# Encoder block on one core: own buffers for the bias tables, result stores by head pair, wider value products

## The chip, the cores and the metric

The kernel runs on one core of a Trainium2 chip. A core has five engines with instruction queues of their own: TensorE (PE; its weight loads are shown apart as PEld), VectorE (DVE), ScalarE (ACT), GpSimd (POOL) and SyncE (SP, which here issues most DMAs). PE writes to PSUM, eight banks of 512 float32 columns in each of 128 partitions; the other memory on the core is SBUF. The metric is the time of one execution on the device in microseconds; lower is better.

## The reference, cut to what matters

One layer of an encoder: 2048 tokens, width 1024. After a norm, one projection feeds two attention mixers; their outputs are normed, concatenated and projected, and an expert layer and a last norm follow. The change lies in the two mixers and in what prepares them.

```python
# mixer A: 8 heads x 64, three patterns (window, dilation) = (128,1), (512,4), (2048,16)
rel_steps = np.arange(span)[None, :] - half_steps - np.arange(qb)[:, None]
bias = rel_bias[t5_relative_bucket(rel_steps * dilation)].transpose(2, 0, 1)
scores = where(valid, q @ k.T * dh ** -0.5 + bias, NEG_INF)      # keys i + j*dilation, |j| <= 64
m, p = max(scores), exp(scores - max(scores)); l = sum(p)
o, lse = p @ v / l, m + log(l)
out_a = sum over patterns of softmax(lse over patterns) * o
# mixer B: 8 heads, every query against every key
sc = (q_nope @ k_nope.T + q_rope @ k_rope.T) * 96 ** -0.5
out_b = softmax(sc) @ v
```

## The kernel before, in words

Products that need float32 accuracy are made of two halves: a value is split into a high part and its residue (the low part), and high x high, high x low and low x high are added up in PSUM. The order of instructions on every engine is the order in which the program emits them.

**Phase 1** (`phase1`) goes over 16 token tiles of 128 tokens. For tile c the loop emits `stage_b(c + 1)` (eight transposes of the normed tile into PSUM, ACT takes the high part, DVE the residue, L153 to L156), `stage_a(c + 3)` (the norm: ACT's squares, some ten small DVE instructions, one DVE scaling, L136 to L141, and the load of x two tiles on), steps of work done on the side, and `stage_c(c)` (24 products of 416 columns for mixer B's latents, L163). The transposes use the PSUM pool `pt` of two banks, the projections `pm` of four.

Work on the side: `bias_tables` builds mixer A's biases. After a load step and a one-hot step it makes eight tables for pattern 1 (`y`, 496 columns each, two per step), two parts for pattern 4 (384 and 288 columns) and one for pattern 16 (256). Each table is two products of 8 rows (L397, L398) into a bank of `pt`, a DVE copy to an SBUF area `b` (L399) and a store to DRAM by SP; the pattern-1 results alternate between two slots of `b`. `vb_scale` loads mixer B's value weights and works out a power-of-two scale for them; `vscale` does so for mixer A's. `chain` makes one sequence of `bias_tables` and `vb_scale`, and a dictionary says how many steps of it a tile takes: one at tiles 0, 2, 6 and 7, two at 3, 4, 5 and 8. The one-hot tables lie in the columns 1024 to 2048 of `hT[0]`, which later tiles fill.

Then come the v and the q and k projections, held in `hT`, with stores to DRAM.

**Mixer A** (`phase3`) takes the 8 heads one after the other, 20 units a head: 4 of pattern 16, then 8 of pattern 1, then 8 of pattern 4. It is a pipeline over steps s, where a unit passes through `qk` (PE), `soft1` (DVE: adds the bias and takes the row minimum of the negated scores into column 65 of the result tile, L604), `soft2` (POOL subtracts it), `soft3` (ACT's exp), `trans` (PE, ACT), `low` (DVE) and `pv` (PE; ACT then copies the values and the sum of weights of a group of units into columns 0 to 64 of the result tile, L685), each a step after the one before; `pv` runs five steps behind `qk`. At unit 1 of a head SP is given the loads of the next head's q and k (six loads of 0.5 MB), at unit 5 of an even head the v of the next pair.

The result tile `st` holds a head's 48 windows, 66 columns each, from a pool of two buffers. When `pv` has done a head's last unit, which is step 4 of the next head, SP gets eight stores of that head (L723 to L728) into DRAM `na`, where a token's row in a pattern is 8 heads x 66 numbers: every piece is 264 bytes long. A new tile from a pool waits until everything that used the buffer before is done, stores included; `soft1` at the start of a head waits so on DVE.

**Mixer B** (`mla`) works in 256 steps, each with two key tiles for 512 queries of a head: six score products of 512 columns, two products for a later row maximum (DVE reduces it, L796), two ACT exps, residues on DVE and POOL (L833, L834), and the value products, two steps' worth at every second step. For each of 2 key tiles and 4 query tiles there are three: the high weights with the values' 65 columns (64 high parts and a one, L848), the same weights with the 64 low parts (L850), the low weights with the 65 (L852); all three add into the same 65 columns of one bank. After eight steps ACT copies the bank (260 columns) to `os`, DVE works out the reciprocal of the sum, POOL multiplies into `ob`, and SP stores it (L855 to L862).

## Time and profile before

| | us |
|---|---|
| median of the runs shown | 2385.11 |
| lowest and highest of them | 2384.35, 2390.85 |
| the profiled execution | 2390.16 |
| its span, first to last instruction | 2388.1 |

| stretch of the profiled execution | us |
|---|---|
| phase 1, token tiles | 0 to 150 |
| phase 1, v, q and k projections | 150 to 440 |
| mixer A | 440 to 750 |
| mixer B with its preparation | 750 to 1578 |
| output projection, router, experts, last norm | 1578 to 2388 |

The profile is one execution on the chip. Busy times of engines are sums over instructions; of TensorE it also tells the clock granted to it, as a share of full speed, where 1.00 is 2.4 GHz and 0.50 is 1.2 GHz. A releaser, the event that ended an engine's wait, is inferred from semaphore events; where an instruction waits for several things, the last of them by the profile is named, and this can be another than the one that really held it.

### The profile page before, as it was taken

Reading aid. Unit: us, or ns where it says so; the run is one execution under the profiler, and the core shown is the slowest. Engines: PE = TensorE matmul, PEld = TensorE weight load, DVE = VectorE, ACT = ScalarE, POOL = GpSimd, SP = SyncE. Lnnn points to the kernel's source line nnn. Section 1 sums busy time; section 2 is a strip of 40 time slices with the busy share of each in tenths; the row PEclk is TensorE's granted clock in tenths of the full one; section 3 lists DMA queues with packets and bytes.
Section 4 is the critical chain, followed back from the end, with each engine's and each line's share of the span. In section 5 each row is a group of like instructions: output and inputs, shape, how many; then the busy total and the mean of one; then the engine's idle time right before and its main releaser. Section 6 shows DMA issues by size and latency. Waiting matters only on the chain. (4 is left out here: it accounts for less than half of the span.)

```text
span 2388.1 us, 45937 instructions
## 1 busy us (share of the span) xinstructions
PE 2156.3 (90%) x17613; PEld 1826.4 (76%) x17613; DVE 1624.7 (68%) x3584; ACT 1358.1 (57%) x2103; POOL 1075.7 (45%) x1137
## 2 busy tenths in 40 slices
PE   6799998788799999999999999989898799999990
PEld 5689886688788788888888887777676588788870
DVE  6542211457677788888888889877887677777764
ACT  4331111568678577777777776844343376667763
POOL 0110000346465245555555547454654666677740
PEclk8899999979789899999999999989999899999995
DMA  4322446999999300000000022135444598899978
GB/s 140 116 73 66 165 181 170 202 209 160 180 154 140 105 19 6 22 22 6 22 12 15 21 52 87 42 90 169 143 143 168 168 313 277 295 295 324 313 208 299
DMA packets 221776, 333.99 MB, mean 140 GB/s; under 512 B 113849, under 2 KB 165986, under 8 KB 205476
## 3 DMA queue, kind: packets, MB, share of 16 engines
q1 hardware_dynamic: 191508, 195.41, 32.9%
q0 software_dynamic: 29760, 134.85, 17.6%
q8 instruction: 140, 2.29, 0.4%
q14 instruction: 80, 0.66, 0.1%
q10 hardware_dynamic: 288, 0.79, 0.1%
HBM read 248.24 MB, written 109.64 MB: 150 GB/s over the span
## 5 line engine op out<-in xcount | busy, mean ns | idle before, releaser
L834 POOL TENSOR_TENSOR lo<-p,hi 128x512 f16<-128x512 f32 x256 | 359.1, 1403 | 315.8 <-ACT p L828 310.2
L796 DVE TENSOR_REDUCE part<-M 128x1 f32<-128x512 f32 x512 | 347.3, 686 | 50.6 <-PE M L794 48.1
L827 ACT ACTIVATE hi<-S 128x1024 f16<-128x1024 f32 x256 | 261.9, 1023 | 209.7 <-PE S L822 209.5
L828 ACT ACTIVATE p<-S 128x1024 f32<-128x1024 f32 x256 | 261.0, 1019 | 0.0
L833 DVE TENSOR_TENSOR lo<-p,hi 128x512 f16<-128x512 f32 x256 | 204.2, 798 | 9.8
L848 PEld LDWEIGHTS <-hi 128*128 128x128 f16 x2048 | 190.0, 97 | 26.2 <-issue 25.8
L852 PE MATMUL O<-VB,lo 128*128 128x65 f16 x2048 | 204.9, 193 | 5.4 <-DVE lo L833 3.1
L848 PE MATMUL O<-VB,hi 128*128 128x65 f16 x2048 | 206.4, 194 | 0.0
L850 PE MATMUL O<-VB,hi 128*128 128x64 f16 x2048 | 205.6, 196 | 0.0
L620 POOL TENSOR_TENSOR pp<-sb,st 128x512 f32<-128x512 f32 x32 | 33.4, 1049 | 363.3 <-DVE st L604 357.1
L852 PEld LDWEIGHTS <-lo 128*128 128x128 f16 x2048 | 191.5, 100 | 6.0 <-DVE lo L833 3.6
L850 PEld LDWEIGHTS <-hi 128*128 128x128 f16 x2048 | 191.4, 97 | 0.3
L626 POOL TENSOR_TENSOR pp<-sb,st 128x256 f32<-128x256 f32 (+1 forms) x256 | 143.0, 580 | 51.7 <-DVE st L604 41.7
L1972 DVE TENSOR_TENSOR s<-raw,s 128x1024 fp32r<-128x1024 f32 x120 | 140.1, 1220 | 12.8 <-ACT s L1970 12.6
L1929 PE MATMUL pd<-s,hT 128*128 128x512 f32 x540 | 138.3, 404 | 1.7 <-ACT hT L1916 1.7
L2016 POOL DMA_INDIRECT d_x<-o,rec x47 | 90.6, 1928 | 105.3 <-ACT s L1970 28.1
L1280 PE MATMUL pm<-s,mT_hi 128*128 128x512 f32 x512 | 135.2, 411 | 0.0
L303 DVE SCALAR_TENSOR_TENSOR qk_sb<-pm,qkscale,qk_sb 128x512 fp32r<-128x512 f32 x32 | 24.0, 751 | 162.8 <-ACT qk_sb L302 156.5
L654 ACT ACTIVATE phi<-PT 128x512 f16<-128x512 f32 (+1 forms) x160 | 96.0, 600 | 53.6 <-PE PT L643 52.4
L1929 PEld LDWEIGHTS pd<-s,hT 128*128 128x128 f32 x540 | 101.2, 188 | 30.1 <-issue 4.3
L578 PE MATMUL S<-KA,QA 128*128 128x256 f32 (+2 forms) x384 | 117.4, 329 | 7.5 <-issue 7.5
L604 DVE CUSTOM_DVE_ANT_0 sb<-S,t 128x128 f32<-128x128 f32 (+1 forms) x240 | 72.4, 349 | 75.5 <-PE S L579 37.7
(467 smaller groups left out, 6390.3 us busy)
## 6 DMA issues: line engine op xcount, KB each, us to landing
x<-in_x SPq DMA_DIRECT2D x32, 512.0 KB
d_qk<-qk_sb SPq DMA_DIRECT2D x64, 256.0 KB
na<-d_na SPq DMA_DIRECT2D x48, 264.0 KB
QA<-d_qk SPq DMA_DIRECT2D x16, 512.0 KB
KA<-d_qk SPq DMA_DIRECT2D x16, 512.0 KB
KB<-d_qk SPq DMA_DIRECT2D x16, 512.0 KB
d_x<-x SPq DMA_DIRECT2D x16, 512.0 KB
d_h<-h SPq DMA_DIRECT2D x16, 512.0 KB
```

The source lines that it names most:

```text
L626: nc.gpsimd.tensor_sub(dst, src, st[h][:, s0 + i, 65:66, None, None].to_broadcast([128, 2, na, nx // 2]))
L796: nc.vector.tensor_reduce(part[m][:, qt, kc:kc + 1], ps, axis=AX.X, op=ALU.max)
L827: nc.scalar.activation(hi, ps, AF.Exp)
L828: nc.scalar.activation(p32, ps, AF.Exp)
L833: nc.vector.tensor_sub(lo[:, :, 0:LV], p32[:, :, 0:LV], hi[:, :, 0:LV])
L834: nc.gpsimd.tensor_sub(lo[:, :, LV:512], p32[:, :, LV:512], hi[:, :, LV:512])
L848: nc.tensor.matmul(o[:, qt], hi[:, j, q], V[:, 0:65], start=(kt == 0 and qt == 0), stop=False, skip_group_check=True)
L850: nc.tensor.matmul(o[:, qt, 0:64], hi[:, j, q], V[:, 65:129], start=False, stop=False, skip_group_check=True)
L852: nc.tensor.matmul(o[:, qt], lo[:, j, q], V[:, 0:65], start=False, stop=(kt == 15 and qt == 3), skip_group_check=True)
L1280: nc.tensor.matmul(ps[half], mT[a][:, j], wo[b][j // 2][:, j % 2, 512 * half:512 * half + 512], start=(n == 0), stop=(n == 23))
L1929: self.nc.tensor.matmul(ps[:, half], hT[a][:, j], w[b][:, j, 512 * half:512 * half + 512], start=(n == 0), stop=(n == len(k) - 1))
L1972: eng.tensor_sub(lo, src, hi)
```

## The change

Three edits that touch different stretches.

First, the bias tables take their PSUM from a pool of their own, `p1tb`, two banks, and their steps are one per tile at tiles 0 and 2 to 8 (the tables themselves fall on tiles 3 to 8; with the one-hot step at tile 2 this is seven tiles). The four steps of `vb_scale` go beside them, at tiles 2, 4, 5 and 6, and still use `pt`. The pattern-1 results alternate among four slots of `b`, and the pattern-4 and pattern-16 results move within it. The one-hot tables lie from column 1280 on, since they are read up to tile 8. The fetch of the first value weights at tile 8 is emitted after the table step.

Second, mixer A's results are kept for a head pair and a pattern: a tile [128, 16 windows, 2 heads, 66] for each of the three patterns, one buffer each, in the same SBUF space as before. `put` stores a pattern when `pv` has done its last unit in the odd head: pattern 16 at step 8 of the odd head (one store), pattern 1 at step 16 (three), pattern 4 at step 4 of the next head (four). A piece in DRAM is 2 x 66 numbers, 528 bytes.

Third, in mixer B the three first query tiles take their 65 columns and the 64 low parts in one product of 129 columns, each query tile having 129 columns of the bank; the fourth keeps two products, since the bank has 512 columns. The copy to `os` takes 452 columns, POOL adds the low sums to the high ones for three query tiles, and the multiplication is done in place in `os`.

```diff
--- before.py
+++ after.py
...
             vs = vscale()
-            ahead = chain(self.bias_tables(rawp, hT[0][:, :, 1024:2048], pt), self.vb_scale(rawp, pt, sm))
+            tb = c1.enter_context(tc.tile_pool(name="p1tb", bufs=2, space=PSUM))
+            tables = self.bias_tables(rawp, hT[0][:, :, 1280:2048], tb)
+            vb = self.vb_scale(rawp, pt, sm)
...
+                if c in (10, 11, 12, 13, 14):
+                    next(vs, None)
+                if c in (0, 2, 3, 4, 5, 6, 7, 8):
+                    next(tables, None)
+                if c in (2, 4, 5, 6):
+                    next(vb, None)
                 if c == 8:
                     fetch(0)
                     fetch(1)
-                if c in (10, 11, 12, 13, 14):
-                    next(vs, None)
-                for _ in range({0: 1, 2: 1, 3: 2, 4: 2, 5: 2, 6: 1, 7: 1, 8: 2}.get(c, 0)):
-                    next(ahead, None)
...
         for y in range(8):
-            sl = b[:8, (y % 2) * 496:(y % 2) * 496 + 496]
+            sl = b[:8, (y % 4) * 496:(y % 4) * 496 + 496]
             table(o1[:, 0:31, 7 - y:23 - y], 496, sl)
             nc.sync.dma_start(AP(dr["t1"], y * 496, [[8 * 496, 8], [1, 496]]), sl)
             if y % 2:
                 yield
...
-        v4 = b[:8, 1000:1672]
+        v4 = b[:8, 0:672]
...
-        v16 = b[:8, 1700:1956]
+        v16 = b[:8, 992:1248]
...
-            ot = ctx.enter_context(tc.tile_pool(name="p3o", bufs=2))
+            ot = ctx.enter_context(tc.tile_pool(name="p3o", bufs=1))
...
-            SLOT = {pw: n for n, pw in enumerate((pat, w) for pat in (16, 4, 1) for p, ws in units if p == pat for w in ws)}
+            SLOT = {(pat, w): n for pat in (16, 4, 1) for n, w in enumerate(w for p, ws in units if p == pat for w in ws)}
...
+            def results(h, pat):
+
+                if (h // 2, pat) not in st:
+                    st[h // 2, pat] = ot.tile([128, 16, 2, 66], F32, name=f"st{pat}")
+                return st[h // 2, pat][:, :, h % 2]
+
+            def put(p, pat):
+
+                so = st.pop((p, pat)).rearrange("p w h n -> p w (h n)")
+                out = lambda w0, step, n: AP(dr["na"], w0 * 128 * 528 + p * 132, [[528, 128], [step * 128 * 528, n], [1, 132]])
+                if pat == 16:
+                    nc.sync.dma_start(out(0, 1, 16), so)
+                elif pat == 4:
+                    for i, t in enumerate((0, 3, 1, 2)):
+                        nc.sync.dma_start(out(16 + t, 4, 4), so.rearrange("p (r t) n -> p r t n", t=4)[:, :, i])
+                else:
+                    nc.sync.dma_start(out(33, 1, 14), so[:, 2:16])
+                    nc.sync.dma_start(out(32, 1, 1), so[:, 0:1])
+                    nc.sync.dma_start(out(47, 1, 1), so[:, 1:2])
 
...
-                if h not in st:
-                    st[h] = ot.tile([128, 48, 66], F32, name="st")
+                res = results(h, pat)
...
-                        accum_out=st[h][:, SLOT[pat, w], 65:66])
+                        accum_out=res[:, SLOT[pat, w], 65:66])
...
-                                         st[h][:, s0:s0 + nw, 65:66].to_broadcast([128, nw, n]))
+                                         res[:, s0:s0 + nw, 65:66].to_broadcast([128, nw, n]))
...
-                    nc.scalar.activation(st[h][:, idx:idx + nw, 0:65], ps[:, :nw], AF.Copy)
+                    nc.scalar.activation(results(h, pat)[:, idx:idx + nw, 0:65], ps[:, :nw], AF.Copy)
...
                     h, u = divmod(s - 5, U)
-                    if u == U - 1:
-                        so = st.pop(h)
-                        out = lambda w0, step, n: AP(dr["na"], w0 * 128 * 528 + h * 66, [[528, 128], [step * 128 * 528, n], [1, 66]])
-                        nc.sync.dma_start(out(0, 1, 16), so[:, 0:16])
-                        for i, t in enumerate((0, 3, 1, 2)):
-                            nc.sync.dma_start(out(16 + t, 4, 4), so[:, 16:32].rearrange("p (r t) n -> p r t n", t=4)[:, :, i])
-                        nc.sync.dma_start(out(32, 1, 1), so[:, 32:33])
-                        nc.sync.dma_start(out(47, 1, 1), so[:, 33:34])
-                        nc.sync.dma_start(out(33, 1, 14), so[:, 34:48])
+                    if h % 2 and u in (3, 11, 19):
+                        put(h // 2, {3: 16, 11: 1, 19: 4}[u])
...
-                    state["O"] = psO.tile([128, 4, 65], F32, name="O")
+                    state["O"] = psO.tile([128, 512], F32, name="O")
...
+
                         q = slice(128 * qt, 128 * qt + 128)
-                        nc.tensor.matmul(o[:, qt], hi[:, j, q], V[:, 0:65], start=(kt == 0 and qt == 0), stop=False,
-                                         skip_group_check=True)
-                        nc.tensor.matmul(o[:, qt, 0:64], hi[:, j, q], V[:, 65:129], start=False, stop=False,
-                                         skip_group_check=True)
-                        nc.tensor.matmul(o[:, qt], lo[:, j, q], V[:, 0:65], start=False, stop=(kt == 15 and qt == 3),
-                                         skip_group_check=True)
+                        c0 = 129 * qt
+                        own = 129 if qt < 3 else 65
+                        nc.tensor.matmul(o[:, c0:c0 + own], hi[:, j, q], V[:, 0:own], start=(kt == 0 and qt == 0),
+                                         stop=False, skip_group_check=True)
+                        if own == 65:
+                            nc.tensor.matmul(o[:, c0:c0 + 64], hi[:, j, q], V[:, 65:129], start=False, stop=False,
+                                             skip_group_check=True)
+                        nc.tensor.matmul(o[:, c0:c0 + 65], lo[:, j, q], V[:, 0:65], start=False,
+                                         stop=(kt == 15 and qt == 3), skip_group_check=True)
                 if kp == 7:
-                    os = wk.tile([128, 4, 65], F32, name="os", bufs=1)
-                    nc.scalar.activation(os, o, AF.Copy)
+                    os = wk.tile([128, 4, 129], F32, name="os", bufs=1)
+                    nc.scalar.activation(os.rearrange("p a n -> p (a n)")[:, 0:452], o[:, 0:452], AF.Copy)
+                    nc.gpsimd.tensor_add(os[:, 0:3, 0:64], os[:, 0:3, 0:64], os[:, 0:3, 65:129])
                     rl = sm.tile([128, 4, 1], F32, name="rl")
                     nc.vector.reciprocal(rl, os[:, :, 64:65])
                     nc.vector.tensor_scalar(rl, rl, vinv, None, op0=ALU.mult)
-                    ob = wk.tile([128, 4, 64], F32, name="ob", bufs=1)
-                    nc.gpsimd.tensor_mul(ob, os[:, :, 0:64], rl.to_broadcast([128, 4, 64]))
+                    ob = os[:, :, 0:64]
+                    nc.gpsimd.tensor_mul(ob, ob, rl.to_broadcast([128, 4, 64]))
                     nc.sync.dma_start(AP(dr["ob"], 4 * n * 128 * 512 + h * 64, [[512, 128], [128 * 512, 4], [1, 64]]), ob)
```

## Rows read from the trace of the kernel before

**Rows 1.** The page's second part, the span in 40 slices of 59.7 us each: busy tenths of PE, the granted TensorE clock in tenths of full speed, and the share of the DMA engines.

```profile
PE   6799998788799999999999999989898799999990
PEclk8899999979789899999999999989999899999995
DMA  4322446999999300000000022135444598899978
```

**Rows 2.** Stretches of the token-tile loop of phase 1, cut where the projections of tiles 2, 5, 9 and 12 begin (33.6, 80.4, 109.2 and 125.3 us). Columns: stretch and its length, busy time of PE, PEld, DVE, ACT and POOL (with instruction counts), granted clock, DMA share, GB/s.

```profile
33.60:80.40 46.80, 29.57 (x121) 21.95 (x119) 25.55 (x68) 12.47 (x34) 5.08 (x24) 0.75 0.22 66
80.40:109.20 28.80, 24.39 (x132) 23.20 (x131) 14.84 (x47) 11.77 (x35) 3.38 (x18) 0.93 0.33 100
109.20:125.30 16.10, 16.10 (x98) 15.87 (x96) 12.89 (x44) 12.66 (x28) 3.36 (x18) 1.00 0.82 269
```

**Rows 3.** PE in order of time, 40 to 66 us: table products (L397 and L398). Columns: start and duration in us, line, what; in brackets the idle time before it and its releaser.

```profile
41.99 0.42 PE L397 MATMUL pT<-hT_hi 33*8 33x496 f32 x1 [2.77 <-DVE hT_lo L156]
...
42.59 0.42 PE L397 MATMUL pT<-hT_hi 33*8 33x496 f32 x1
...
46.66 0.58 PE L397 MATMUL pT<-hT_hi 33*8 33x496 f32 x1 [3.39 <-DVE raw L399]
...
63.23 0.58 PE L397 MATMUL pT<-hT_hi 33*8 33x496 f32 x1 [3.72 <-DVE raw L399]
```

**Rows 4.** DVE in order of time, 38 to 90 us, the same columns: the first instruction of a norm chain (L46), the scaling by it (L141), the copies of a pair of tables (L399), and the residues of two transposes (L156).

```profile
42.46 0.14 DVE L46 TENSOR_SCALAR rs_t<-ss 128x1 f32<-128x1 f32 x1
...
44.74 1.28 DVE L141 SCALAR_TENSOR_TENSOR xn<-x,ss,g_attn 128x1024 f32<-128x1024 f32 x1
45.95 1.24 DVE L399 COPY raw<-pT 8x496 f32<-8x496 f32 x2
50.10 1.24 DVE L399 COPY raw<-pT 8x496 f32<-8x496 f32 x2 [2.92 <-DMA d_t<-raw]
57.49 1.29 DVE L156 TENSOR_TENSOR hT_lo<-pT,hT_hi 128x512 fp32r<-128x512 f32 x2 [6.15 <-ACT hT_hi L155]
```

**Rows 5.** Stretches of mixer A, columns as in rows 2: head 0; then (from a table of the heads one after the other, 441.0 to 745.8 us) head 6, head 7 and the sum; then, from a table without the idle time at heads' starts, heads 2 and 3.

```profile
441.00:486.80 45.80, 30.69 (x345) 29.04 (x345) 24.70 (x113) 25.70 (x51) 21.86 (x36) 0.82 1.06 210
...
679.90:714.20 34.30, 31.97 (x389) 31.31 (x390) 27.12 (x117) 25.44 (x53) 22.09 (x36) 0.82 1.02 121
714.20:745.80 31.60, 29.13 (x413) 27.79 (x411) 28.79 (x118) 28.88 (x60) 21.32 (x35) 1.00 1.06 142
sum 304.80, PE 256.97 PEld 248.44 DVE 216.38 ACT 223.91 POOL 175.55; mean PE 32.12 PEld 31.06 DVE 27.05 ACT 27.99 POOL 21.94
525.50:557.30 31.80, 29.98 (x387) 29.20 (x387) 27.16 (x116) 24.97 (x53) 21.75 (x36) 0.89 1.16 134
561.20:590.20 29.00, 27.77 (x393) 26.64 (x392) 27.06 (x116) 26.72 (x57) 21.67 (x36) 1.00 1.11 228
```

**Rows 6.** DVE in order of time: the first bias addition (L604) of heads 2, 3, 4 and 6, with the idle time before it and its releaser as the trace infers it, and, between them in time, the first one of pattern 4 in head 3 (step 12 of that head).

```profile
525.50 0.29 DVE L604 CUSTOM_DVE_ANT_0 sb<-S,t 128x128 f32<-128x128 f32 x1 [3.49 <-DMA QA<-d_qk]
...
561.27 0.29 DVE L604 CUSTOM_DVE_ANT_0 sb<-S,t 128x128 f32<-128x128 f32 x1 [4.03 <-DMA d_na<-st]
...
579.44 0.36 DVE L604 CUSTOM_DVE_ANT_1 sb<-S,t 128x192 f32<-128x192 f32 x1
...
611.78 0.29 DVE L604 CUSTOM_DVE_ANT_0 sb<-S,t 128x128 f32<-128x128 f32 x1 [21.59 <-DMA QA<-d_qk]
...
679.85 0.29 DVE L604 CUSTOM_DVE_ANT_0 sb<-S,t 128x128 f32<-128x128 f32 x1 [5.45 <-DMA QA<-d_qk]
```

**Rows 7.** What the DMA queues moved in five stretches of mixer A: 592 to 607 us (DVE idle ahead of head 4), 540 to 552 (264-byte stores), 514 to 520 (264-byte stores), 560 to 572 (v loads, pieces of 520 bytes), 576 to 584 (q and k loads, pieces of 8192 bytes).

```profile
DMA packets 4162, 1.22 MB, mean 81 GB/s; under 512 B 4143, under 2 KB 4143, under 8 KB 4143
...
DMA packets 3502, 0.91 MB, mean 76 GB/s; under 512 B 3501, under 2 KB 3501, under 8 KB 3501
...
DMA packets 3174, 0.83 MB, mean 138 GB/s; under 512 B 3173, under 2 KB 3173, under 8 KB 3173
...
DMA packets 5964, 3.08 MB, mean 257 GB/s; under 512 B 72, under 2 KB 5963, under 8 KB 5963
...
DMA packets 293, 1.76 MB, mean 220 GB/s; under 512 B 54, under 2 KB 80, under 8 KB 80
```

**Rows 8.** SP's DMA issues in order of time, 420 to 640 us: start and the time that SP took for them. The first and the last store of head 2.

```profile
575.09 0.52 SPq L723 DMA_DIRECT2D d_na<-st  x1
...
597.98 0.73 SPq L728 DMA_DIRECT2D d_na<-st  x1
```

**Rows 9.** The steady stretch of mixer B, columns as in rows 2; and, from the instructions grouped by line and shape (busy us, mean ns of one, idle before), two of mixer A: a POOL operation on 192 columns and an ACT copy of 390 columns out of PSUM.

```profile
840.00:1440.00 600.00, 599.66 (x7023) 504.47 (x7022) 498.74 (x875) 437.01 (x504) 311.31 (x237) 1.00 0.09 23
...
L626 POOL TENSOR_TENSOR pp<-sb,st 128x192 f32<-128x192 f32 x80 | 38.9, 507 | 9.7 <-DVE st L604 7.8
...
L685 ACT ACTIVATE st<-O 128x390 f32<-128x390 f32 x32 | 15.7, 490 | 0.4
```

**Rows 10.** PE in order of time: the first of 48 value products in a row and the score product behind them (mixer B), and eight 128-column transposes with the projection behind them (phase 1). A duration holds the way through the array; what one costs is the distance of the starts.

```profile
951.52 0.20 PE L848 MATMUL O<-VB,hi 128*128 128x65 f16 x1
...
953.00 0.48 PE L820 MATMUL S<-Qh,Kh 97*128 97x512 f32 x1
...
113.78 1.04 PE L153 MATMUL pT<-ident,xn 128*128 128x128 f32 x8
114.57 1.75 PE L163 MATMUL pm<-wc_hi,hT_hi 128*128 128x416 f32 x8
```

More of the change, by code (lines that the diff above doesn't have):

```diff
@@ L618, in soft2 @@
                 n = na * nx
+                res = results(h, pat)
                 if pat == 16:
                     nc.gpsimd.tensor_sub(pp.rearrange("p (w x) -> p w x", w=nw), sb.rearrange("p (w x) -> p w x", w=nw),
-                                         st[h][:, s0:s0 + nw, 65:66].to_broadcast([128, nw, n]))
+                                         res[:, s0:s0 + nw, 65:66].to_broadcast([128, nw, n]))
                     return
@@ L625, in soft2 @@
                     src = sb[:, i * n:i * n + n].rearrange("p (a h x) -> p h a x", h=2, a=na)
-                    nc.gpsimd.tensor_sub(dst, src, st[h][:, s0 + i, 65:66, None, None].to_broadcast([128, 2, na, nx // 2]))
+                    nc.gpsimd.tensor_sub(dst, src, res[:, s0 + i, 65:66, None, None].to_broadcast([128, 2, na, nx // 2]))
             def soft3(s):
```

## The prediction

> **What bounds the kernel now.** I read the slices of the page first. The mixer-B stretch (about 840 to 1440 us) shows PE full at granted clock 9 of 10; two stretches ahead of it do not: the token tiles at the start and mixer A (about 440 to 750 us), where PE is partly idle, the clock falls and, in mixer A, the DMA line stands at 9 [rows 1]. Each part of the change lies in one of these three stretches, so each is costed in its own.
>
> The token tiles: three tile periods with table steps, from tile 2's projection to tile 5's, took 46.8 us, the next four 28.8 us, and three later ones 16.1 us, or 5.4 us each at a full clock [rows 2]. In PE's order of time one sees why: the first table product waits 2.77 us for DVE to read a transpose out of the shared PSUM pair, and the third waits 3.39 us in one tile and 3.72 us in another for DVE's copy [rows 3]. In DVE's order the second pair of copies waits about 3 us for the store of the first (two result slots), and then DVE stands 6.15 us because PE's projection, and so the next transposes, came late [rows 4]. The mean clock there was 0.75 [rows 2].
>
> Mixer A: the eight heads took 304.8 us, an undisturbed one 29.0 us, with PE, DVE and ACT all about 27 us busy; the last took 31.6 us, with extra preparation [rows 5]. DVE idles 3.49, 4.03, 21.59 and 5.45 us at the starts of heads 2, 3, 4 and 6 [rows 6]. The trace names a QA load as releaser of three of them, but look at what the queue moved: while DVE stood from 590.2 to 611.8, the packets of 592 to 607 were nearly all under 512 bytes, the 264-byte stores, at 81 GB/s [rows 7]. The QA load had landed. Head 4 writes its row minima into the result tile that head 2 used, so it waits for head 2's stores; SP issued these from 575 to 599, behind the v loads and the next q and k [rows 8].
>
> Mixer B: in 599 of 600 us PE is busy; DVE 499, ACT 437 and POOL 311 [rows 9].
>
> **Part 1, tables.** The number of products, copies and stores is the same; two table steps per tile become one, their PSUM comes from a pair that transposes do not use, and results have four slots. What stays: PE's own time. A table's two products start 0.60 us before the next table's [rows 3], so a pair of tables costs 1.2 us; four pairs, the pattern-4 tables (672 columns of 992, 0.8 us) and the pattern-16 one (0.3 us) make 5.9 us. The seven periods then take 7 x 5.4 = 37.6 us, plus 5.9, plus the 28.8 - 21.5 = 7.3 us by which the four later periods exceed 5.4 us, mostly the scale step of mixer B's values. It keeps the old PSUM pair and is only moved to earlier tiles, so I leave it whole: 50.8 us. Before: 75.6. **Gain 25 us.** The cover: DVE needs 1.3 (residues) + 2.3 (norm chain) + 1.2 (scaling) + 1.2 (copies) = 6.0 us a tile [rows 4], below PE's 6.6. If the excess of 7.3 goes as well, the gain is 32; if only the waits of the third table in each of the three tiles go, 3.39 and 3.72 us in the two whose rows are shown [rows 3], it is 11. On SP the table stores stand ahead of a later x load, which is two tiles ahead of its use (11 us); the value-weight fetch at tile 8 now stands behind the last table's store in SP's order, some 3 us, and its first reader comes two tiles later. Both at nothing.
>
> **Part 2, result stores.** 49,152 pieces of 264 bytes become 24,576 of 528, the same 13 MB, in three waves per head pair of 2048 pieces, 1.08 MB each. The tile of a pattern has one buffer: pattern 16's wave goes out at step 8 of the odd head, pattern 1's at step 16, pattern 4's at step 4 of the next even head, and that head writes the same tiles at steps 0, 4 and 12. If no wait were left, mixer A would be 45.8 (head 0 with the first loads, untouched) + 35.2 (head 1 to 522.0) + 5 x 29.0 + 31.6 = 257.6 us, 47.2 less [rows 5, 6].
>
> What is late next is the wave. Its time w is bounded by four rows [rows 7]: 264-byte stores went at 138 GB/s (3174 packets in 6 us) and elsewhere at 76; 520-byte loads at 257. So w = 3.9 us if a piece costs what a 264-byte piece costs at its best, 7.8 if a byte does, 4.2 at the speed of the 520-byte loads, 14.2 at the slow speed. I take 6.0, between the first two, which are stores in the same queue. The queue serves in order. The q and k load of 3.15 MB takes 14.3 us at 220 GB/s [rows 7] and is issued about 1.5 us before an even head starts; pattern 4's wave stands behind it and needs some 1.5 us to be seen. It is there at 14.3 + w after the head's start, and step 12 comes at 18.2 (579.44 - 561.27) [rows 6]: a wait of w - 3.9 = 2.1 us in the second pair. In the third and fourth pair, pattern 1's wave, issued some 3.3 us before the head starts, delays the load too: 2w + 12.5 - 18.2 = 6.3 us each. Behind this wait stand DVE's next steps and the residues that the value products need; after such waits at their starts of 3.49, 4.03 and 5.45 us heads took 31.8, 29.0 and 34.3 us, PE's clock being down after the first and the third [rows 5, 6], so I add 2.5 us each for two of them. **Gain** 47.2 - 2.1 - 12.6 - 5 = **27 us**; at w = 4.2 it is 40, at 7.8 it is 16, at 14.2 waits at steps 0 and 4 (19 us) join in and it is a loss of 39. SP issues half as many stores; the v load stands behind one wave of 1.08 MB where it stood behind a head's 1.62 MB.
>
> A rule on this, beside the 264-byte rows at 76 and 138 GB/s: the Trainium skill, "DMA: Bandwidth & Descriptors", section "Latency and other measured facts", says that transfers need 512 bytes for line rate and that below it the engine reads, modifies and writes. The rows fit it as far as they go; no row here shows a store of 528 bytes. What it would make of the time is rival (e).
>
> **Part 3, value products.** For three of four query tiles the 65- and the 64-column product on the same weights become one of 129: 3 x 16 x 32 = 1536 products and weight loads go. 48 products took 953.00 - 951.52 = 1.48 us, 30.9 ns each [rows 10]. At the 2.4 GHz that the granted clock of 1.00 stands for, 64 more columns are 26.7 ns, so the wide product costs 57.6 against 61.8: 4.2 ns x 1536 = **6.5 us**, all of it on PE, which is the bound. Bounds: 0, if only columns count and the gap is tied to them, and 8.1 ns each (12 us) if 129 columns take 53.75 ns. Added: ACT's copy of 452 columns for 260 (390 columns took 490 ns [rows 9]; some 0.2 us more, 32 times) and a POOL addition of 192 columns (507 ns [rows 9], 16 us in all), both once in eight steps, on engines with a quarter and half of their time free [rows 9]. The next value product on that bank comes only behind two steps' scores and maxima. POOL's next residue is queued behind the addition; its reader is more than a step away. At nothing; without that cover, 0.7 us each, 22 us.
>
> **Sum.** 25 + 27 + 6.5 = 59 us off the profiled execution of 2390.2 us (span 2388.1) gives 2331. The median of the runs shown is 5 us lower, 2385.1; the forecast against it is **2326 us**. Nothing behind mixer A gives the time back: mixer B is held by PE, and its inputs are loaded ahead.
>
> **Rivals.** (a) *The single-buffered pattern tile becomes the wait.* Its place is step 12 of heads 2, 4 and 6, on DVE. For it: the queue is at 9 [rows 1] and went at 76 GB/s for 12 us [rows 7]. Against it: the first stores of a burst were at the faster speed. At w = 14.2: 2385 - 25 + 39 - 6.5 = 2393. It decides from w of some 13, where its loss eats the other two gains. Chance 0.04. (b) *The queue stays the bound of mixer A* (w near 10): the waits move and sum up to the same 47 us; 2354. Chance 0.12. (c) *Part 1 does only half*: DVE frees the new PSUM pair late, behind the norm chain, and the clock stays low; with a gain of 11, 2341. For it: 6.0 against 6.6 us is a thin cover. Chance 0.15. (d) *Wide products are paced by more than their columns.* The 128-column transposes take 99 ns each (8 in 0.79 us [rows 10]); at that pace 1536 x 37 ns = 57 us are added, 2390. Against it: those are four-byte weights, and the two-byte ones of [rows 10] are loaded every 30.9 ns. Chance 0.03. (e) *Stores of 528 bytes go at the speed of the 520-byte loads*, w = 4.2, and mixer A gains 40: 2313. For it: both move in the same queue between the same memories; against it, a store is the other direction. Chance 0.14. By the Trainium skill's rule under part 2 ("DMA: Bandwidth & Descriptors") it would come out so.
>
> On (d) the Trainium skill, "TensorE: Matmul & The Clock Gate", section "Back-to-back issue gap", gives 81 ns for a sustained 128-column product. By it the part would cost 1536 x 19 ns = 30 us (an estimate from the page), 2362 us; the rows at 30.9 ns for 65 columns do not bear it out.
>
> **How the numbers follow.** Forecast 0.50; (a) to (e) 0.48; 0.02 for what I don't see. A measurement of this kernel can tell about 0.3%, 7 us. Faster: forecast, (b), (c), (e) and a share of the unseen: 0.92; same 0.04 with (d); slower 0.04 with (a). The range goes from 2385 - 32 - 40 - 12 = 2301, taken as 2302, to a little above (b), 2362, so that (c) and (b) lie in it and (a), (d) and (b) with (c) do not.
>
> **What would show it.** Part 1: tile periods of 6 to 7 us from tile 2 on, no table product waiting over 1 us, the clock at full from 33 to 110 us; wrong if a product still waits for a copy. Part 2: no idle DVE at head starts after head 1, waits of 2 to 6 us at the first pattern-4 step of heads 2, 4, 6; packets of 528 bytes at about 180 GB/s. Wrong if heads still take over 33 us. Part 3: mixer B's 600 us shorter by 5 to 6 us with PE still full; wrong if DVE waits for the added step.

## The result, and the profile after

| | before | after |
|---|---|---|
| median, us | 2384.73 (4 runs) | 2330.07 (4 runs, 2323.88 to 2334.11) |
| ratio, 95% interval | | 0.9765, 0.9734 to 0.9797 |
| profiled execution, span | 2390.16, 2388.1 | 2334.11, 2332.3 |

The forecast was 2326. The stages begin and end at instructions that both kernels have; divided there, the 55.8 us by which the two spans differ lie here:

| stretch | forecast gain | gain |
|---|---|---|
| token tiles, up to the last tile's projection | 25 | 18.0 |
| v, q and k projections | 0 | -0.4 |
| mixer A, from DVE's first wait for scores to the end of its last bias addition (305.8 before, 276.6 after) | 27 | 29.2 |
| preparation of mixer B, from mixer A's last residue on | 0 | 2.9 |
| mixer B, first row-maximum product to last copy of results | 6.5 | 3.9 |
| all behind it | 0 | 2.2 |

The page's slices of the kernel after, 58.3 us each, answer to [rows 1]: the granted clock is higher in the token tiles, and the slices in which it stood at 7 in mixer A are gone.

```profile
PE   6899998799999999999999999888888899999990
PEclk9999999889999899999999999999999999999995
DMA  4312536999955100000000131145534699899978
```

The token tiles after, cut where the projections of tiles 2, 5, 9, 12 and 14 begin; columns as in [rows 2].

```profile
32.94:60.65 27.71, 23.68 (x113) 19.94 (x112) 19.30 (x53) 12.97 (x36) 5.08 (x24) 0.88 0.38 123
60.65:89.20 28.55, 26.12 (x141) 23.20 (x140) 21.41 (x67) 10.55 (x32) 3.36 (x18) 0.94 0.28 90
89.20:105.36 16.16, 16.16 (x99) 15.93 (x98) 12.09 (x38) 12.78 (x28) 3.38 (x18) 1.00 0.85 269
105.36:125.20 19.84, 14.41 (x70) 13.53 (x68) 9.49 (x21) 7.44 (x24) 4.54 (x18) 0.83 0.06 22
```

The three periods that took 46.8 us take 27.7, the next four 28.6 for 28.8 us, which is the same. PE in order of time shows what is left: the table products (L401) no longer wait for a transpose or a copy [rows 3], but for the one-hot step and, in two tiles, for the next tile's high parts on ACT; the scale steps' products (L317) and the transposes behind them (L153) wait for a bank of `pt`. The last row is part of a projection at half clock, eight products in 3.12 us; at full clock they take 1.75 [rows 10].

```profile
40.63 0.42 PE L401 MATMUL pT<-hT_hi 33*8 33x496 f32 x1 [2.06 <-DVE hT_hi L395]
...
49.95 0.42 PE L401 MATMUL pT<-hT_hi 33*8 33x496 f32 x1 [0.98 <-ACT hT_hi L155]
...
59.29 0.42 PE L401 MATMUL pT<-hT_hi 33*8 33x496 f32 x1 [0.98 <-ACT hT_hi L155]
...
67.99 0.66 PE L153 MATMUL pT<-ident,xn 128*128 128x128 f32 x4 [2.15 <-DVE hT_lo L156]
...
114.28 0.58 PE L317 MATMUL pT<-vmax,ones 128*128 128x2 f32 x2 [3.29 <-DVE hT_lo L156]
114.72 3.12 PE L163 MATMUL pm<-wc_hi,hT_hi 128*128 128x416 f32 x8
```

Mixer A's heads 1, 2, 3, 4 and 6 after, from first bias addition to first bias addition (columns as in [rows 5]); then DVE in order of time, the waits that are left there, which answer to [rows 6].

```profile
468.36:503.94 35.58, 35.50 (x419) 34.77 (x418) 27.31 (x116) 27.93 (x58) 22.00 (x36) 0.80 1.02 222
503.94:539.94 36.00, 32.33 (x418) 31.20 (x417) 27.25 (x117) 28.23 (x60) 22.05 (x37) 0.91 1.13 231
539.94:569.52 29.58, 29.24 (x418) 28.37 (x417) 27.12 (x116) 27.86 (x60) 22.02 (x37) 1.00 0.73 177
569.52:605.62 36.10, 31.61 (x418) 30.54 (x417) 27.25 (x117) 28.23 (x60) 22.05 (x37) 0.91 1.12 228
...
635.32:667.44 32.12, 29.50 (x418) 28.51 (x417) 27.09 (x117) 28.01 (x60) 22.05 (x37) 1.00 0.65 138
```

```profile
526.22 0.36 DVE L627 CUSTOM_DVE_ANT_1 sb<-S,t 128x192 f32<-128x192 f32 x1 [3.69 <-DMA d_na<-st]
...
592.62 0.36 DVE L627 CUSTOM_DVE_ANT_1 sb<-S,t 128x192 f32<-128x192 f32 x1 [4.50 <-DMA d_na<-st]
...
656.54 0.36 DVE L627 CUSTOM_DVE_ANT_1 sb<-S,t 128x192 f32<-128x192 f32 x1 [2.63 <-DMA d_na<-st]
```

All three are pattern 4's first bias addition (192 columns), step 12 of heads 2, 4 and 6, and now the releaser is the store itself. What the queues moved in two waves, 555.6 to 559.8 and 584.4 to 591.8 us ([rows 7] for the 264-byte stores): the first wave had the queue to itself, 261 GB/s; beside the second ran the v load.

```profile
DMA packets 2060, 1.10 MB, mean 261 GB/s; under 512 B 16, under 2 KB 2059, under 8 KB 2059
...
DMA packets 2752, 1.45 MB, mean 197 GB/s; under 512 B 77, under 2 KB 2747, under 8 KB 2747
```

Mixer B after: a steady stretch (columns as in [rows 9]); the stretch of 384 row-maximum reductions (L813), six heads, and the 64 after them, with DVE's busy time in these alone, clock, DMA share and GB/s; and PE at a group of value products, first product and the score product behind it ([rows 10]).

```profile
795.00:1390.00 595.00, 594.21 (x5762) 498.00 (x5761) 511.42 (x874) 439.06 (x502) 319.09 (x265) 1.00 0.09 26
```

```profile
813.70:1354.45 540.75, 259.60 (x384) 1.00 0.08 21
1354.45:1451.80 97.35, 43.35 (x64) 0.98 0.18 57
```

```profile
901.14 0.23 PE L868 MATMUL O<-VB,hi 128*128 128x129 f16 x1
...
902.56 0.48 PE L837 MATMUL S<-Qh,Kh 97*128 97x512 f32 x1
```

The same two stretches before (there the reductions are at L796):

```profile
863.27:1409.04 545.77, 260.82 (x384) 1.00 0.08 21
1409.04:1505.62 96.58, 43.42 (x64) 1.00 0.19 58
```

The six heads take 5.0 us less, the stretch behind them 0.8 us more. In the steady stretch PE is busy for 594 of 595 us, as it was before.

### The profile page after: what moved, and what is told of

It reads as the page before. It is cut to its first block, busy times and chain, and to the rows that moved or that the text cites. A ratio compares the mean times of both kernels' runs of the same rounds, so it can differ in the third digit from the quotient of the medians.

```text
span 2332.3 us, 42859 instructions
## 1 busy us (share of the span) xinstructions
PE 2132.7 (91%) x16077; PEld 1805.7 (77%) x16077; DVE 1636.1 (70%) x3584; ACT 1361.2 (58%) x2103; POOL 1089.9 (47%) x1169
## 5 line engine op out<-in xcount | busy, mean ns | idle before, releaser
L851 POOL TENSOR_TENSOR lo<-p,hi 128x512 f16<-128x512 f32 x256 | 353.5, 1382 | 310.4 <-ACT p L845 308.1
L813 DVE TENSOR_REDUCE part<-M 128x1 f32<-128x512 f32 x512 | 346.3, 685 | 32.5 <-PE M L811 30.5
L850 DVE TENSOR_TENSOR lo<-p,hi 128x512 f16<-128x512 f32 x256 | 218.1, 853 | 7.0 <-ACT p L845 0.2
L873 PE MATMUL O<-VB,lo 128*128 128x65 f16 x2048 | 197.6, 193 | 6.9 <-DVE lo L850 4.6
L868 PEld LDWEIGHTS <-hi 128*128 128x128 f16 x2048 | 182.7, 98 | 24.8 <-issue 23.2
L868 PE MATMUL O<-VB,hi 128*128 128x129 f16 (+1 forms) x2048 | 198.3, 215 | 0.0
L873 PEld LDWEIGHTS <-lo 128*128 128x128 f16 x2048 | 177.3, 99 | 8.1 <-DVE lo L850 5.4
L1992 ACT ACTIVATE s<-raw 128x1024 fp32r<-128x1024 f32 x120 | 118.6, 1051 | 12.5 <-DMA raw<-in_w_gate,eidx 6.0
L306 ACT ACTIVATE qk_sb<-pm,qkscale 128x512 fp32r<-128x512 f32 x32 | 22.0, 688 | 167.2 <-DMA d_qk<-qk_sb 115.1
L1302 PEld LDWEIGHTS pm<-s,mT_hi 128*128 128x128 f32 x512 | 96.9, 195 | 21.9 <-ACT mT_hi L1287 0.5
```

What stands on the lines that cost most here:

```text
L813: nc.vector.tensor_reduce(part[m][:, qt, kc:kc + 1], ps, axis=AX.X, op=ALU.max)
L850: nc.vector.tensor_sub(lo[:, :, 0:LV], p32[:, :, 0:LV], hi[:, :, 0:LV])
L851: nc.gpsimd.tensor_sub(lo[:, :, LV:512], p32[:, :, LV:512], hi[:, :, LV:512])
L868: nc.tensor.matmul(o[:, c0:c0 + own], hi[:, j, q], V[:, 0:own], start=(kt == 0 and qt == 0), stop=False, skip_group_check=True)
L873: nc.tensor.matmul(o[:, c0:c0 + 65], lo[:, j, q], V[:, 0:65], start=False, stop=(kt == 15 and qt == 3), skip_group_check=True)
L1302: nc.tensor.matmul(ps[half], mT[a][:, j], wo[b][j // 2][:, j % 2, 512 * half:512 * half + 512], start=(n == 0), stop=(n == 23))
```

## The experiments

The theory was that the three edits work in stretches of their own and add up; rivals and sizes stand with each run. Ratios are to the kernel before on the same chip, with 95% intervals; runs 1 to 4, 5 to 8 and 9 to 12 were measured on three chips, where the kernel before took 2387.26, 2381.24 and 2386.40 us. The diffs show the lines that matter and are shortened.

**1 to 3, one edit alone.** The edit of each is the part of the change's diff that its name tells, for example for the third:

```diff
+nc.tensor.matmul(o[:, c0:c0 + own], hi[:, j, q], V[:, 0:own], ...)   # with its 129-column os; tables and stores as before
```

> The kernel before with the first edit alone. The changed kernel's token tiles gained 18 us where 25 were forecast. If the three edits act each in its own stretch, this gives 2385 - 18 = 2367 us and the v projections begin 18 us earlier. Rival: the shift of phase 1 is taken back or enlarged in mixer A, whose loads collide with other work; then it is off 2367 by over 5 us, with mixer A longer or shorter than 305 us.

Measured: 2366.49, 0.9912 (0.9877 to 0.9946). The token tiles end 18.3 us earlier, as in the whole change, and mixer A lasts 308.5 us, so the shift is neither taken back nor enlarged there.

> The kernel before with the second edit alone. Additive theory: mixer A from the first bias addition to the last residue about 29 us shorter (309.8 to about 281), mixer B's preparation 3 us shorter, 2385 - 32 = 2353 us, with waits of 3 to 5 us on DVE at step 12 of heads 2, 4 and 6. Rival: part of the 29 us came from the other edits' shift; then mixer A is 285 us or longer.

Measured: 2353.17, 0.9855 (0.9823 to 0.9888). In the stretch of the table mixer A takes 277.6 us, 28.2 less than before; step 12 waits 3.91, 4.99 and 2.51 us.

> The kernel before with the third edit alone. By the forecast 25 ns a step come off where PE is the bound: 0.8 us a head in seven heads, nothing in the last, where the next stage's preparation runs beside it: 5.6 us, 2379 us. Rival: the added ACT and POOL work costs as much as the products save, within 1 us of 2385.

Measured: 2382.73, 0.9977 (0.9955 to 0.9999). The 384 reductions take 540.50 us, 5.3 less, but the 64 behind them 97.75, 1.2 more. The median's gain of 4.5 us is hardly more than such a comparison can tell; the stretch tells it. The three gains by medians, 20.8 + 34.1 + 4.5 = 59, stand beside 54.7 for the whole; by their own stretches they are 18.3, 28.2 and 4.1 us beside 18.0, 29.2 and 3.9. No edit needs another.

**4, the changed kernel with pieces of 264 bytes.** Tiles, buffers and the moments of storing stay; each wave becomes two sets of stores.

```diff
-so = st.pop((p, pat)).rearrange("p w h n -> p w (h n)")    # pieces [1, 132]
+for e in range(2): so = sp[:, :, e]                         # pieces [1, 66]
```

> The changed kernel with the same three waves at the same steps, each wave written as two sets of 264-byte pieces, one for each head. Theory of the forecast: the length of a piece sets the wave's time; at the rates of 264-byte stores seen before (138 and 76 GB/s) a wave takes 8 to 14 us, the waits at step 12 grow from 3.6 us to 8 to 20 us, others come back at heads' starts, and mixer A loses 15 to 50 us against the changed kernel: 2345 to 2380 us. Rival: what freed the heads' starts was that a pattern is stored early and by itself, and the length of a piece is nothing; then within 5 us of 2330.

Measured: 2378.65, 0.9973 (0.9954 to 0.9993). What the queues moved from 521 to 536 us, a wave of which the v load takes a part, and DVE's waits from 470 to 700 us (engine, line and releaser; us in total, times, longest):

```profile
DMA packets 5318, 1.92 MB, mean 128 GB/s; under 512 B 4231, under 2 KB 5283, under 8 KB 5283
```

```profile
DVE sb L629 <- DMA d_na<-st: 33.8, 4, 13.8
...
DVE sb L629 <- DMA v<-d_va: 14.8, 1, 14.8
```

48.6 us of waits where the changed kernel has 10.8; the last of them, put down to the v load, ended when the wave had landed. The twelve waves last 9.5 to 18.8 us, 13.2 in the mean. Mixer A takes 319.0 us, more than the 305.8 before, since the tile with one buffer is still there. So not fewer or earlier waves but the length of a piece carries part 2; the rival falls.

**5, a load moved behind pattern 4's wave.**

```diff
-if u == 1 and h + 1 < HA:
+if u == (5 if h % 2 == 0 and h else 1) and h + 1 < HA:
```

> The changed kernel, but in heads 2, 4 and 6 the load of the next head's q and k is issued at step 5 and not at step 1, behind pattern 4's wave of the pair before. Wait: the load that delays pattern 4's wave is that of the odd head, so it is this one that must stand behind the wave. Theory (step 12 waits because the wave stands in the queue behind 3.15 MB of loads): the waits of 3.69, 4.50 and 2.63 us at step 12 go or fall below 1 us, with some of the half clock behind them; mixer A's scores to last step 265 to 270 us instead of 276.6, whole time 2318 to 2324. Rival (the wave itself is what lasts, whatever stands ahead of it): the waits stay within 1 us of these values; 2328 to 2333. Second rival (the late load makes the odd head wait for its q and k): waits of several us at the starts of heads 3, 5, 7; 2330 or more.

Measured: 2334.60, 0.9806 (0.9774 to 0.9838). Heads 2, 3 and 4 (columns as in [rows 5]):

```profile
500.36:532.31 31.95, 29.51 (x418) 28.54 (x417) 27.12 (x117) 28.39 (x60) 22.07 (x37) 1.00 0.77 168
532.31:567.61 35.30, 35.17 (x418) 34.44 (x417) 27.23 (x117) 27.94 (x58) 22.05 (x36) 0.81 1.07 231
567.61:599.98 32.37, 29.51 (x418) 28.52 (x417) 27.12 (x117) 28.39 (x60) 22.06 (x37) 1.00 0.78 168
```

```profile
531.18 0.30 PE L603 MATMUL S<-KB,QA 128*128 128x128 f32 x1 [2.10 <-DMA KB<-d_qk]
532.31 0.29 DVE L627 CUSTOM_DVE_ANT_0 sb<-S,t 128x128 f32<-128x128 f32 x1 [2.65 <-PE S L603]
...
599.98 0.29 DVE L627 CUSTOM_DVE_ANT_0 sb<-S,t 128x128 f32<-128x128 f32 x1 [3.08 <-PE S L603]
```

The second rival: step 12 waits for no store any more, but heads 3 and 5 start 2.65 and 3.08 us late (the time lies in the rows of heads 2 and 4): DVE waits for scores, and PE for the q and k that they need. Head 3 then runs at a clock of 0.81. The wait moved; mixer A lasts 277.9 us.

**6, the tables' step ahead of the next tile's transposes.**

```diff
 for c in range(NT):
+    if c in (0, 2, 3, 4, 5, 6, 7, 8): next(tables, None)
     if 0 < c < NT - 1: stage_b(c + 1)
-    if c in (0, 2, 3, 4, 5, 6, 7, 8): next(tables, None)
```

> The changed kernel with the tables' step of a token tile issued ahead of the next tile's normalisation and high parts. Theory (the table products wait 1 to 2 us a tile for the next tile's high parts, which ACT writes into the same buffer in which the one-hot scratch lies): tile periods from tile 2 to 9 fall from 56.3 to 45 to 51 us, whole time 2319 to 2325. Rival (DVE's chain of residues, norm and copies sets the period, and the order changes nothing): 55 to 58 us, whole time 2327 to 2333.

Measured: 2325.23, 0.9754 (0.9717 to 0.9790). Tile 2 to tile 9, columns as in [rows 2]:

```profile
33.24:82.12 48.88, 46.40 (x252) 39.78 (x250) 40.58 (x120) 24.11 (x66) 8.95 (x42) 0.97 0.39 122
```

48.9 us where the changed kernel took 56.3; no table product waits. The theory's size holds in its stretch; the whole time is just above the range written. That the false dependence is its cause is tested by run 9.

**7, the scales' broadcasts in the tables' pair.**

```diff
-self.pow2_scale(sm, pt, am, float(D), vsc, dr["va_inv"]); vb = self.vb_scale(rawp, pt, sm)
+self.pow2_scale(sm, tb, am, float(D), vsc, dr["va_inv"]); vb = self.vb_scale(rawp, tb, sm)
```

> The changed kernel with the broadcast products of the two value scales in the tables' PSUM pair and no longer in the pair of the transposes. Theory (these products wait 2.15, 3.29 and 2.15 us for a PSUM buffer that transposes hold): the waits fall below 1 us and the time from tile 12 to tile 14 from 19.9 us to 16 to 17, whole time 2322 to 2327. Rival (the products wait for their own input, DVE's reduction, and would wait in any PSUM buffer): no change, 2328 to 2333.

Measured: 2335.13, 0.9793 (0.9764 to 0.9822). Stretches from tile 4 to 6 and from tile 12 to 14; then PE's two longest waits of the first:

```profile
51.12:79.80 28.68, 17.05 (x75) 13.89 (x74) 15.60 (x44) 7.48 (x22) 2.25 (x12) 0.76 0.21 64
115.52:126.51 10.99, 10.99 (x69) 10.83 (x68) 8.57 (x19) 6.01 (x20) 3.17 (x12) 1.00 0.11 40
```

```profile
63.57 0.56 PE L317 MATMUL pT<-vbmax,ones 128*128 128x2 f32 x2 [4.62 <-DVE raw L403]
...
78.88 0.58 PE L401 MATMUL pT<-hT_hi 33*8 33x496 f32 x1 [5.04 <-DVE raw L403]
```

Both: where no table is near, the theory's gain is larger than written (11.0 us for 19.8); between the tables, broadcast and tables now wait for each other in the pair, and two periods that took 18.8 us take 28.7. The two effects cancel: the whole time is that of the changed kernel, above both ranges written.

**8, runs 5, 6 and 7 together.**

> The load behind the wave, the tables' step first and the scales in the tables' PSUM pair, all three in the changed kernel. If each theory holds the gains add up, as they lie in different stretches: 10 + 8 + 5 = 23 us, 2303 to 2311. If only one of them holds, 2318 to 2325; if none, 2327 to 2333.

Measured: 2324.01, 0.9756 (0.9726 to 0.9786). The token tiles end at 115.6 instead of 134.5 us: with the tables first, the pair is free for the broadcasts. The moved load takes some back: mixer A lasts 279.9 us for 276.6, and a wait of 4.7 us for a store is there again, now at the start of head 3. By these stretches the three save 18.9 - 3.3 = 15.6 us, and the profiled execution is 13.4 us shorter than that of the changed kernel; the medians differ by 6 only. That is the size written down for one edit that holds, but two of the three hold: the tables' order, and with it the scales in the tables' pair.

**9, the one-hot scratch in rows 3 and 7.**

```diff
-oh = [hi[:33, i] for i in range(3)];            rbh, rbl = hi[:33, 3, 0:8], hi[:33, 3, 16:24]
+oh = [hi[:33, 3], hi[:33, 7], o16[:33]];        rbh, rbl = hi[:33, 3, 744:752], hi[:33, 3, 760:768]
```

> The changed kernel, its order of work untouched, but the one-hot scratch and the split bias values lie in rows 3 and 7 of the high-part buffer and in a small tile of their own, and no longer in rows 0 to 3. The next tile's high parts, which ACT writes to rows 0 to 3 and then 4 to 7 in other columns, share no column with the scratch in either version, but a stretch from the first to the last column of such a copy covers rows 0 to 2 of the old scratch and no part of the new one. Theory (the table products waited for those copies because whole stretches are compared): no table product waits for ACT's high parts, the time from tile 2 to tile 9 falls from 56.3 to 48 to 53 us, whole time 2321 to 2327. Rival (the copies only stood late in the queues, and the order is what counts): the waits stay near 1 us, 55 to 58 us, whole time 2327 to 2333.

Measured: 2331.37, 0.9778 (0.9748 to 0.9809). PE's waits from 33 to 88 us:

```profile
PE pT L153 <- DVE hT_lo L156: 2.2, 1, 2.2
PE pT L402 <- DVE hT_hi L396: 2.0, 1, 2.0
PE pT L318 <- DVE hT_lo L156: 0.6, 1, 0.6
```

No table product waits for ACT any more, though nothing moved in the order: the dependence was a false one. But tile 2 to tile 9 takes 54.7 us for 56.3, outside both intervals written down, and 1.6 us is no more than the scatter: run 5, whose token tiles are those of the changed kernel, takes 54.9. So the dependence cost 1.6 us at most; the waits for the one-hot step and for the scale remain. Order and not this dependence is most of run 6.

**10, two buffers for 12 of pattern 4's 16 windows.**

```diff
-ot.tile([128, 16, 2, 66], F32, name=f"st{pat}")
+[ot.tile([128, 12 - 8 * i, 2, 66], F32, name=f"st4{i}", bufs=2 - i) for i in range(2)]   # pattern 4
```

> The changed kernel with two buffers for the first 12 of the 16 result windows of pattern 4 (the last 4 keep one), no load moved. Theory (step 12 waits for the wave to read the single tile, and nothing else stands there): the waits of 3.69, 4.50 and 2.63 us at step 12 go, with some of the half clock behind two of them; mixer A from its first to its last bias addition 263 to 267 us instead of 276.6, whole time 2317 to 2322. Rival (as with the moved load, the wait only turns up at another place: at the later windows, or at the next heads' starts): 274 to 278 us, whole time 2327 to 2333.

Measured: 2319.01, 0.9725 (0.9696 to 0.9754). Heads 2, 3 and 5:

```profile
498.01:527.66 29.65, 29.33 (x418) 28.47 (x417) 27.15 (x117) 27.90 (x60) 22.04 (x37) 1.00 1.07 232
527.66:557.28 29.62, 29.30 (x418) 28.42 (x417) 27.15 (x117) 27.88 (x60) 22.02 (x37) 1.00 1.03 224
...
586.97:616.89 29.92, 29.45 (x418) 28.46 (x417) 27.10 (x116) 28.07 (x60) 22.02 (x37) 1.00 1.05 225
```

Every head from 2 to 6 takes 29.6 to 29.9 us at full clock, mixer A 260.9 us: the theory. The single tile was the wait, and with room for two the queue keeps up.

**11, runs 6, 7 and 10 together.**

> The tables' step first, both value scales in the tables' PSUM pair (in the three together these two took the token tiles from 134.5 to 115.6 us) and the two buffers for pattern 4, without the moved load. If the buffers do what they should, 19 and 10 to 14 us add up: 2296 to 2303. If the wait only moves, 2309 to 2314.

Measured: 2298.11 (2297.48 to 2301.78), 0.9634 (0.9609 to 0.9659): both gains, and faster than either kernel of this case. Tile 2 to tile 9:

```profile
33.18:79.15 45.97, 44.71 (x252) 38.24 (x250) 40.26 (x120) 23.98 (x66) 8.64 (x42) 1.00 0.41 130
```

**12, the tables back in the transposes' pair.** One step a tile and the four slots stay.

```diff
-tables = self.bias_tables(rawp, hT[0][:, :, 1280:2048], tb)
+tables = self.bias_tables(rawp, hT[0][:, :, 1280:2048], pt)
```

> The changed kernel with the tables' products back in the PSUM pair of the transposes; one table step per tile and the four result slots stay. Theory (the own PSUM pair is what carries part 1): the products and transposes wait for each other again, tile 2 to tile 9 takes 66 to 76 us instead of 56.3, whole time 2340 to 2350. Rival (one step per tile and four slots are enough): 55 to 60 us, whole time 2328 to 2335.

Measured: 2352.92, 0.9859 (0.9829 to 0.9889). PE's waits from 26 to 126 us:

```profile
PE pT L401 <- DVE hT_lo L156: 11.0, 6, 2.8
PE pT L401 <- DVE raw L403: 3.8, 1, 3.8
```

The stretch from tile 2 to tile 9, columns as in [rows 2]:

```profile
33.10:110.00 76.90, 56.16 (x250) 47.25 (x249) 41.35 (x120) 23.49 (x66) 8.43 (x42) 0.80 0.25 78
```

76.9 us, no less than the 75.6 before; this and the whole time lie a little above both ranges written. Without a PSUM pair of the tables' own, spreading and slots bring nothing. Whether the pair alone, without them, would bring the 18 us was not tried.

**The same stretches in all fourteen traces** tell which differences are clear of the scatter (us; the numbers are runs).

| stretch | as before | as changed |
|---|---|---|
| token tiles' end | 152.5 to 153.8 (before, 2, 3) | 130.8 to 135.2 (after, 1, 4, 5, 10) |
| tile 2 to tile 9 | 75.6 to 76.7 (before, 2, 3) | 54.9 to 56.3 (after, 1, 4, 5, 10) |
| tile 12 to tile 14 | 16.3 to 17.7 (before, 2, 3) | 16.5 to 20.2 (after, 1, 4, 5, 10) |
| mixer A | 305.2 to 308.5 (before, 1, 3) | 274.4 to 277.6 (after, 2, 6, 7, 9, 12) |
| preparation of mixer B | 63.2 to 64.1 (before, 1, 3) | 60.3 to 62.9 (after, 2, 5 to 12); 69 (4) |
| mixer B | 764.5 to 765.6 (before, 1, 2) | 759.4 to 762.7 (after, 3 to 12) |

The parts that no run edits move too: the v, q and k projections take 282.0 to 289.4 us, and what stands behind mixer B 804.0 to 812.5. So a difference of a few us between two whole times tells little, where a stretch tells much.

## Why the prediction was right, and where its terms were off

**Part 1: the right mechanism, 18.0 us for 25.** The forecast for tile 2 to tile 9 was 50.8 us, which is 16.1 + 3 x 1.2 = 19.7 for the first three periods and 31.1 for the next four. These took 28.6, less than forecast; the first three took 27.7. The step that was mis-sized is "What stays: PE's own time", 5.4 us a tile and the tables on top: it let the table products follow the transposes at once, and they waited. The first wait, 2.06 us, is for the one-hot step at tile 2, which DVE does behind the norm chain and which the sum of 6.0 us for DVE does not count; the two of 0.98 us are for ACT's copies, by the false dependence of run 9. These 4.0 us are half of the 8.0 us that are missing; some 3.3 us more are projections that ran in part at half clock, in a stretch at 0.88 of full clock where 1.00 was assumed. The half clock does not follow from such a wait each time: behind the first one the projection's three parts took 2.82, 2.22 and 1.67 us here, but 1.77, 1.67 and 1.67 in run 1, with the same tables. With the order turned round (run 6) the term measures 48.9, with the scale out of the transposes' pair too (run 11) 46.0. The prediction's own sign, periods of 6 to 7 us and no table product waiting over 1 us, did not come: the seven periods took 8.8, 9.3, 9.6, 9.2, 7.7, 6.3 and 5.4 us. Rival (c) did not happen by its mechanism, for no table product waits over 0.3 us for a copy; by size the 18 us lie halfway between it and the forecast. From tile 12 to 14, where I had no term, the v scale's steps took 19.8 us for 16.3, their wait 3.29 for 2.64 us, with the projection behind it now at half clock. The table of fourteen traces shows that 16.3 and 19.8 are near the ends of two ranges that overlap, so this part is not shown to come from the change; run 7 takes the wait away.

**Part 2: 29.2 us for 27.** The wave was forecast at 6.0 us; in the trace after, the time from a wave's first to last packet is 4.1 to 7.4, 5.7 in the mean of twelve. The waits at step 12 are 10.8 us where 14.7 was forecast, and heads 2, 4 and 6, with 36.0, 36.1 and 32.1 us against 29.6 undisturbed, lose 15.5, so 4.7 beyond the waits where 5 stood for the clock. The single terms are less good than their sum: 3.7 for 2.1, 4.5 and 2.6 for 6.3 each; that their errors cancel is luck. The "1.5 us to be seen" stands in no row; in the trace after, the three waits ended 1.0, 0.8 and 0.7 us after their wave's last packet. The bounds are looser than they look: at w = 4.2 the terms give 41.5, or 36.5 with the 5 us for the clock, where 40 is written, and at 14.2 a loss of 33 to 35 where 39 is. The sign "wrong if heads still take over 33 us" came out in heads 2 and 4, though the mechanism held: the prediction's own terms make 29.0 + 6.3 + 2.5 = 37.8 us of such a head. The forecast delayed all by packets ahead in one queue; but beside the wave of 584.4 to 591.8 went some 600 packets of the v load, which SP issued behind it (from 581.7 us, the wave at 577.7), and in head 6, without such a load, the wait was the shortest. Runs 4, 5 and 10 settle the mechanism: the wait is the time of the wave, and of the load ahead of it, against a tile with one buffer. Rival (a) is seen in run 4, whose waits of 13 to 15 us take back nearly all; (b) and (e) lie on either side of it. The rule of rival (e) stands in the Trainium skill, "DMA: Bandwidth & Descriptors", section "Specifications": line rate wants transfers of 512 bytes or more, and below that the engine reads, modifies and writes. The trace agrees for a wave that is alone, 261 GB/s as the 520-byte loads, and run 4 for pieces of 264 bytes, whose waves last 9.5 to 18.8 us; but only two of the twelve waves of 528-byte pieces went so fast, and those beside other transfers are slower.

**Part 3: 3.9 us for 6.5.** A group of value products takes 1.42 us for 1.48, twelve products less, 5 ns each for the 4.2 forecast; taken from 36, 24 narrow ones at 30.9 ns leave 57 ns for a wide one, where 57.6 was worked out. Six heads gain 5.0 us, 26 ns a step for 25. Rival (d) falls. The Trainium skill, "TensorE: Matmul & The Clock Gate", section "Back-to-back issue gap", gives 81 ns for a sustained product of 128 columns; the 57 ns measured here for 129 do not bear it out. The added ACT and POOL work is hidden, as costed. What failed is "all of it on PE, which is the bound" for all eight heads. In the stretch where the next stage's preparation runs beside mixer B, PE had not been the bound before either, busy for 92.67 of 96.58 us; there 64 reductions now take 97.35 us at a clock of 0.98 for 1.00, in run 3 alone 97.75 at 0.97. Why the clock falls there was not tried.

**Not forecast: 2.9 us before and 2.2 behind mixer B.** Behind mixer B the kernel before has 809.9 us and after 807.7, inside the 804.0 to 812.5 of code that no run changes, so this is not shown to come from the change. The preparation took 63.2 to 64.1 us in the three traces with the old stores and 60.3 to 62.9 in ten with the new ones; the ranges do not overlap, so a part of the 2.9 us probably comes with the stores, by a path that was not tried.

**Luck in the total.** 2330 is as near to 2326 as it is because 7.0 and 2.6 us less than forecast in parts 1 and 3 meet 2.2 us more in part 2 and some 5 us that no term foresaw.

## What to carry to other kernels

When side work gets PSUM of its own, look next at its place in the engines' order: behind the next tile's work it waits for that work, and a wait of 2 us can bring some us at half clock behind it (here it did in the changed kernel, and did not in run 1). Before a load is moved to shorten a wait for a store, ask what the load feeds; a second buffer for the one tile that waits (6.3 KB a partition here) took the whole wait away, where the moved load only carried it to the next heads' starts. Two moves that each bring little can need each other: scales in the tables' pair cost 10 us between the tables until the tables came first.

## What I had not expected

A table product waited for a copy into columns that it does not read, and the wait went when the scratch changed rows, with the order untouched. A transfer issued behind a wave moved packets before the wave was done (some 600 in 7.4 us). Stores of 528 bytes went as fast as the 520-byte loads when alone (two waves of twelve), 261 against 257 GB/s.
